# Grouped-query attention on one core: the one-block ScalarE tile of three-block jobs in the transposes' PSUM tile

## The chip, the cores and the metric

The kernel runs on one core of one Trainium2 chip. The metric is the device time of one execution in microseconds (us); lower is better. Times quoted for "the runs" are medians over executions on the chip. The profile is that of a single profiled execution, and its times count from the first instruction of the program (the span). PE is the matrix engine (PEld its weight loads), ACT is ScalarE, DVE is VectorE, POOL is GpSimd, and SP issues most of the transfers. PSUM, where PE writes its results, has eight banks of 512 float32 values in each of 128 partitions.

## The reference

Softmax attention for 8 batches, 512 positions, 32 query heads and 8 key/value heads of dimension 64. Four query heads share one key/value head.

```python
scale = 1.0 / np.sqrt(dim)
K_expanded = np.repeat(K, heads_per_group, axis=2)
V_expanded = np.repeat(V, heads_per_group, axis=2)
scores = np.einsum('bhqd,bhkd->bhqk', Q, K_expanded) * scale
weights = np.exp(scores - np.max(scores, axis=-1, keepdims=True))
weights = weights / (np.sum(weights, axis=-1, keepdims=True) + 1e-10)
output = np.einsum('bhqk,bhkd->bhqd', weights, V_expanded)
```

## The kernel before

The kernel computes exp(score) without subtracting the maximum, sums the weights with a column of ones beside V, divides at the end, and checks at the end that the sums lay in bounds (a general path stands by for other data and isn't run here).

The work is cut into 64 jobs, one for each batch and key/value head. A job has four query heads, taken as two pairs i = 0, 1. For each pair there are four chunks kc of 128 keys and two heads m: 16 blocks of scores in all, each 128 keys by 512 queries, which is one PSUM bank. Two matmuls with 64 rows each make the two blocks (m = 0, 1) of one kc.

The exponential of the 16 blocks is shared out. DVE and POOL together take the first blocks of pair 1: two of them in most jobs, three in every even job from job 10 on (`WIDE`, line 37; 27 such jobs, called three-block jobs here; `taken`, line 183). ScalarE takes the rest in tiles of two blocks (`act_tiles`, `act_tile`, lines 186 and 211). A job with two taken blocks has seven two-block tiles, numbered 0 to 6. A three-block job has an odd number left: its tile 4 has one block (pair 1, kc 1, m 1), the others two.

The eight PSUM banks are held by three pools (lines 84 to 86): two score buffers of two banks each for ScalarE's tiles (`s_pool`, names s_ps), one tile of two banks for DVE's blocks and for transposes (`d_pool`, d_ps), and one of two banks for the products with V (`pv_pool`, pv). A pool's buffer is given out again when all that reads it is done. Since there are two score buffers, the scores of a tile wait until ScalarE has read the tile before the last.

DVE's share of the exponential goes through several steps: u, a scaled and shifted int16 copy of the scores (`exp_d`, line 228); f, the low bits of u (`exp_d2`, line 249); g and w, a correction, in most jobs on POOL (lines 241 and 245, from `correction`); and the sum of u and w, whose bits are the result in pt (`exp_d4`, line 262). Where POOL made w, `exp_d4` of a job is placed in the next job.

All instructions are put out in the order in which the program text names them; each engine works through its own in that order. One turn of the loop over jobs (line 411) for job j puts out, on PE: scores of tiles 0 and 1 and of DVE's first two blocks; the products with V of the job before for pair 0, in two halves with tile 2's scores between them; tile 3's scores; then a d_ps tile with, in its bank 0, eight 128x128 transposes of the Q of a later job (`trans_q`, line 158; two jobs ahead in the stretch concerned); tile 4's scores; and then the products of the job before for pair 1 in three pieces (`cut`, line 432) with the scores of tiles 5 and 6 between them. In a job before a three-block job, the third block of DVE for that job is put in bank 1 of the same d_ps tile (line 484). In a three-block job bank 1 isn't used in this stretch.

On DVE the same turn puts out: u; in some jobs a check of V (`check_v`); `norm` of the job before for pair 0 (reciprocal and o_sb, lines 336 and 340); the copy of the transposes to qt (line 167); `exp_d4` of the job before; f of this job; u of the third block where there is one; `norm` of the job before for pair 1. POOL gets the loads of Q, K and V for later jobs and then g and w. ScalarE gets its seven tiles and nothing else. `norm` frees the pv banks for the next products.

Of the kernel before, what the change touches and what calls it, by code (L numbers as in the profile page):

```python
# [11 lines left out]
FP32 = mybir.dt.float32  # L12
# [46 lines left out]
def fast_path(ctx, tc, Q, K, V, out, flag):  # L59
    nc = tc.nc  # L60
    B, S, H, D = Q.shape
# [5 lines left out]
    NPAIR = HPG // 2  # L67
# [16 lines left out]
    s_pool = ctx.enter_context(tc.tile_pool(name="sps", bufs=2, space=PS))  # L84
# [3 lines left out]
    ident = const_pool.tile([128, 128], BF16, name="ident")  # L88
# [9 lines left out]
    kn, qn, kt, qt = {}, {}, {}, {}  # L98

    def load_k(b, lo=0, hi=KV):  # L100
        if b not in kn:
            kn[b] = knat_pool.tile([128, SC, KV, D], BF16, name="k_nat")
        nc.gpsimd.dma_start(  # L103
            out=kn[b][:, :, lo:hi, :],
            in_=K[b, :, lo:hi, :].rearrange("(sc p) g d -> p sc g d", p=128),
        )


    def load_v(b, lo=0, hi=KV, chunks=range(SC)):
        for sc in chunks:  # L110
            nc.gpsimd.dma_start(  # L111
                out=vt[b % 2][:, sc, lo:hi, 0:D],
                in_=V[b, sc * 128:(sc + 1) * 128, lo:hi, :],
            )
# [6 lines left out]
    def load_q(u, cuts=(0, 2 * HPG)):  # L121
        b, gp = divmod(u, GP)
        h0 = gp * 2 * HPG
        qn[u] = qnat_pool.tile([128, SC, 2 * HPG, D], BF16, name="q_nat")
        for lo, hi in zip(cuts[:-1], cuts[1:]):
            nc.gpsimd.dma_start(  # L126
                out=qn[u][:, :, lo:hi, :],
                in_=Q[b, :, h0 + lo:h0 + hi, :].rearrange("(sc p) h d -> p sc h d", p=128),
            )

    def d_tile():
        return d_pool.tile([128, 2, S], FP32, name="d_ps")
# [15 lines left out]
    def dma_k(b):  # L148
        kt[b] = kt_pool.tile([128, 2, GP, S], BF16, name="kt")
        for sc in range(SC):  # L150
            nc.sync.dma_start_transpose(
                out=kt[b][:, 0, :, sc * 128:(sc + 1) * 128],
                in_=kn[b][:, sc, :, :].rearrange("p g d -> p (g d)"),
            )
        for to, of in ((0, 64), (64, 0)):
            nc.sync.dma_start(out=kt[b][to:to + 64, 1, :, :], in_=kt[b][of:of + 64, 0, :, :])

    def trans_q(j, bank, lo=0, hi=NPAIR):
        u, g = divmod(j, 2)
        ps = bank.bitcast(BF16).rearrange("p (i sc c) -> p i sc c", i=NPAIR, sc=SC)  # L160
        for i in range(lo, hi):
            for sc in range(SC):
                h = g * HPG + 2 * i
                nc.tensor.transpose(ps[:, i, sc, :], qn[u][:, sc, h:h + 2, :], ident)  # L164
        if u not in qt:
            qt[u] = qt_pool.tile([128, 2, NPAIR, S], BF16, name="qt")
        return lambda: nc.vector.tensor_copy(  # L167
            out=qt[u][:, g, lo:hi, :], in_=ps[:, lo:hi, :, :].rearrange("p i sc c -> p i (sc c)")
        )

    def check_v(b, sc):
        n = b * SC + sc
        nc.vector.tensor_reduce(  # L173
            out=okv[:, n:n + 1], in_=vt[b % 2][:, sc, :, 0:D], op=ALU.max, axis=AX.XY,
            apply_absolute_value=True,
        )
# [6 lines left out]
    def taken(j):  # L183
        return 3 if WIDE(j) else 2

    def act_tiles(j):
        every = [(i, kc, m) for i in range(NPAIR) for kc in range(SC) for m in range(2)]
        first = DPAIR * SC * 2
        mine = [n for n in range(len(every)) if not first <= n < first + taken(j)]
        groups = [[n for n in mine if n // 2 == h] for h in range(len(every) // 2)]  # L190
        return [[every[n] for n in group] for group in groups if group]
# [3 lines left out]
    def scores(j, ps, i, kc, m):  # L195
        u, g = divmod(j, 2)
        b, gp = divmod(u, GP)
        keys = kt_first[:, gp, :, :] if b == 0 else kt[b][:, :, gp, :]
        nc.tensor.matmul(  # L199
            ps,  # L200
            keys[64 * m:64 * m + 64, g ^ m, kc * 128:(kc + 1) * 128],
            qt[u][64 * m:64 * m + 64, g, i, :],
            start=True,
            stop=True,
        )

    def open_job(j):
        pt = pt_pool.tile([128, NPAIR, SC, 2, S], FP16, name="pt")
        jobs.setdefault(j, {}).update(pt=pt, pv={})

    def act_tile(j, n):
        group = act_tiles(j)[n]
        i, kc, lo = group[0]
        ps = s_pool.tile([128, 2, S], FP32, name="s_ps")
        for _, _, m in group:
            scores(j, ps[:, m, :], i, kc, m)
        nc.scalar.activation(  # L217
            out=jobs[j]["pt"][:, i, kc, lo:, :], in_=ps[:, lo:, :], func=EXP, scale=scale
        )

    def exp_d(j, lo, hi, ps):
        st = jobs.setdefault(j, {})
        if "u" not in st:
            for name, dtype in (("u", I16), ("f", I16), ("g", BF16), ("w", BF16)):
                st[name] = dve_pool.tile([128, 3, S], dtype, name=name + "16")[:, 0:taken(j), :]
        for n in range(lo, hi):
            scores(j, ps[:, n - lo, :], DPAIR, n // 2, n % 2)
        return lambda: nc.vector.tensor_scalar(  # L228
            out=st["u"][:, lo:hi, :], in0=ps[:, 0:hi - lo, :], scalar1=A_U, scalar2=B_U,
            op0=ALU.mult, op1=ALU.add,  # L230
        )


    def by_pool(j):
        return 3 <= j < NJOB - 1
# [166 lines left out]
    bank = d_tile()  # L402
# [4 lines left out]
    bank = d_tile()  # L407
# [3 lines left out]
    for j in range(NJOB):  # L411
        end = j == NJOB - 1
        last = j - 1
        late = last >= 0
        u, g = divmod(j, 2)
        b, gp = divmod(u, GP)
        open_job(j)
        if j == 1:

            nc.gpsimd.tensor_copy(out=gate, in_=jobs[0]["pt"][0:1, 0, SC - 1, 0, 0:1])  # L420
            load_q(2)
            load_q(3)
        if g == 0 and u >= 1 and u + 3 < NU:
            load_q(u + 3)
        if (gp, g) == (1, 0) and b + 1 < B:
            load_k(b + 1)
        if 3 <= 2 * gp + g < 3 + SC and b + 1 < B:
            load_v(b + 1, chunks=(2 * gp + g - 3,))
        if gp == 2 and g == 0 and b + 1 < B:
            dma_k(b + 1)  # L430

        cut = (4, 18) if taken(j) > 2 else (11, 19)
        act_tile(j, 0)
        if j == 0:
            trans_q(0, bank[:, 1, :], 1, NPAIR)()
            act_tile(j, 1)
            exp_d(j, 0, 2, d_tile())()
        else:
            exp_d(j, 0, 2, d_tile())()
            act_tile(j, 1)  # L440

        if j == 8:
            check_v(0, 0)
        if g == (b < B - 1) and j > 1:
            check_v(b, gp)
        if late:
            pv(last, 0, 0, 16)
        act_tile(j, 2)
        if late:
            pv(last, 0, 16, 32)  # L450
            norm(last, 0)
        act_tile(j, 3)

        reads = []
        if not end:
            bank = d_tile()

            ahead = (j + 1,) if j < 7 else (8, 9) if j == 7 else (j + 2,)
            for n, to in enumerate(ahead):
                if to < NJOB:  # L460
                    reads.append(trans_q(to, bank[:, n, :]))
            if j == 1:
                for swap in range(2):
                    reads.append(first_k(1, swap, bank[:, 1, swap * S // 2:]))
            elif j > 1 and b == 0 and gp + 1 < GP:
                reads.append(first_k(gp + 1, g, bank[:, 1, :]))
        else:
            pv(j, 0, 0, 16)
        for read in reads:
            read()  # L470

        if late and by_pool(last):
            exp_d4(last)
        check_sums()
        exp_d2(j)
        if not by_pool(j):
            exp_d3(j, nc.vector)
            exp_d4(j)
        act_tile(j, 4)
        if late:  # L480
            pv(last, 1, 0, cut[0])
        act_tile(j, 5)
        if not end and taken(j + 1) > 2:
            exp_d(j + 1, 2, taken(j + 1), bank[:, 1:2, :])()
        if late:
            pv(last, 1, *cut)
        act_tile(j, 6)
        if late:
            pv(last, 1, cut[1], 32)
            norm(last, 1)  # L490
            del jobs[last]
        if end:
            pv(j, 0, 16, 32)
            norm(j, 0)
            pv(j, 1, 0, 32)
            norm(j, 1)
# [118 lines left out]
```

## Time and profile before

| | us |
|---|---|
| median of 3 runs | 423.73 |
| lowest and highest of them | 423.38, 423.77 |
| span of the profiled execution | 422.0 |

The profile's page gives the busy time of each engine, then groups of instructions by line, engine and operation with their count, their busy time, the mean length of one in ns, and the idle time of the engine in front of them with what ended it ("<-"). The timeline of an engine lists instructions in order of time as start, length in us, line, operation, output and input tile, and merges equal ones that follow each other ("x14"; the length is then that of the whole stretch). Records of one engine can overlap: the next one begins before the last one has ended, and the idle time counts only stretches that no record covers. Line numbers are those of the kernel before.

The mean clock that PE was granted over the span is 0.984 of the full one.

### The profile page before, as it was taken

The numbers are of one execution on the slowest core, as the hardware profiler recorded it, in microseconds if no ns is written. First come the engines' busy times: TensorE is split into PE (matmuls) and PEld (weight loads), VectorE is DVE, ScalarE is ACT, GpSimd is POOL, SyncE is SP. The second block draws the span as 40 slices with busy tenths as digits, with TensorE's granted clock in tenths as the row PEclk, the third lists the DMA queues.
The fourth block names the chain that finished last, engine by engine and source line by source line (L and its number), as shares of the span: only waits on it lengthen the run. The fifth ranks groups of instructions, "written<-read, shape, count | busy, mean of one in ns | idle before, by whom it ended". The sixth has DMA issues, their size and how long they took to land.

```text
span 422.0 us, 13063 instructions
## 1 busy us (share of the span) xinstructions
PE 385.7 (91%) x5689; PEld 233.6 (55%) x5689; DVE 344.9 (82%) x611; ACT 404.2 (96%) x449; POOL 291.8 (69%) x209
## 2 busy tenths in 40 slices
PE   6889999999999999999999999999999999999983
PEld 2446565555555555555555555555555555555552
DVE  2697788889888888888888888888989888898875
ACT  3899999999999999999999999999999999999992
POOL 8504656778758876787866887677885887666560
PEclk9599999999999999999999999999999999999998
DMA  9996986599967998499964999649996799642223
GB/s 97 177 139 159 217 165 151 70 207 187 191 151 99 216 198 160 133 198 133 229 150 116 206 163 255 157 69 200 157 225 155 122 206 207 148 123 101 102 91 115
DMA packets 91438, 66.95 MB, mean 159 GB/s; under 512 B 52080, under 2 KB 74608, under 8 KB 91376
## 3 DMA queue, kind: packets, MB, share of 16 engines
q0 software_dynamic: 56544, 25.17, 51.1%
q1 hardware_dynamic: 34832, 40.90, 34.5%
q8 instruction: 45, 0.74, 0.7%
q14 instruction: 17, 0.14, 0.1%
HBM read 50.33 MB, written 33.55 MB: 199 GB/s over the span
## 4 chain that ended last, share of the span: by engine, by line
ACT 54%; PE 36%; DVE 6%; issue 1%; POOL 1%; ACTq 0%; DVEq 0%; POOLq 0%
ACT pt L217 54%; PE s_ps L199 17%; PE pv L293 16%; PE d_ps L199 1%; DVE o_sb L340 1%; PE d_ps L164 1%; DVE pt L262 1%; DVE u L228 1%; DVE qt L167 1%; DVE w L245 0%; POOL q_nat L126 0%; DVE kt_first L146 0%; ACTq L217 0%; PE d_ps L143 0%; DVE f L249 0%
## 5 line engine op out<-in xcount | busy, mean ns | idle before, releaser
L217 ACT ACTIVATE pt<-s_ps 128x1024 f16<-128x1024 f32 (+1 forms) x448 | 402.9, 1066 | 9.1 <-PE s_ps L199 9.0
L293 PEld LDWEIGHTS <-pt 128*128 128x128 f16 x4096 | 144.2, 98 | 86.8 <-issue 50.4
L293 PE MATMUL pv<-v,pt 128*128 128x65 bf16 x4032 | 183.2, 195 | 2.6 <-DVE o_sb L340 1.6
L199 PE MATMUL s_ps<-qt,kt 64*128 64x512 bf16 x757 | 152.7, 384 | 19.9 <-ACT pt L217 15.4
L245 POOL TENSOR_TENSOR w<-g,f 128x1024 bf16<-128x1024 bf16 (+1 forms) x60 | 153.7, 2562 | 5.0
L241 POOL TENSOR_SCALAR g<-f 128x1024 bf16<-128x1024 int16 (+1 forms) x60 | 73.9, 1231 | 110.1 <-DVE f L249 110.1
L228 DVE TENSOR_SCALAR u<-d_ps 128x1024 int16<-128x1024 f32 (+1 forms) x91 | 96.2, 1058 | 1.1 <-PE d_ps L199 1.1
L340 DVE TENSOR_TENSOR o_sb<-pv,inv 128x512 f32<-128x512 f32 x125 | 86.5, 692 | 4.5 <-DVE inv L336 0.2
L199 PEld LDWEIGHTS <-kt 64*128 64x128 bf16 x896 | 49.0, 93 | 62.6 <-issue 35.0
L336 DVE RECIPROCAL inv<-pv 128x8 f32<-128x8 f32 x125 | 25.9, 207 | 55.8 <-PE pv L293 55.4
L262 DVE TENSOR_TENSOR pt<-u,w 128x1536 uint16<-128x1536 int16 (+1 forms) x64 | 50.9, 795 | 0.2
L167 DVE COPY qt<-d_ps 128x1024 bf16<-128x1024 bf16 (+1 forms) x65 | 44.3, 683 | 4.5 <-PE d_ps L164 2.9
L164 PE MATMUL d_ps<-ident,q_nat 128*128 128x128 bf16 x512 | 40.1, 222 | 1.1 <-DVE kt_first L146 0.9
L164 PEld LDWEIGHTS <-q_nat 128*128 128x128 bf16 x512 | 29.2, 98 | 15.8 <-issue 15.7
L199 PE MATMUL d_ps<-qt,kt 64*128 64x512 bf16 x139 | 31.4, 376 | 0.3
L249 DVE TENSOR_SCALAR f<-u 128x1536 int16<-128x1536 int16 (+1 forms) x64 | 30.8, 481 | 0.0
L111 POOL DMA_DIRECT2D v<-in_V_dram x32 | 29.0, 910 | 0.4 <-issue 0.4
L126 POOL DMA_DIRECT2D q_nat<-in_Q_dram x34 | 27.4, 806 | 1.5 <-DMA q_nat<-in_Q_dram 1.3
L199 PE MATMUL s_ps<-qt,kt_first 64*128 64x512 bf16 x112 | 23.7, 419 | 4.1 <-ACT pt L217 3.0
L173 DVE TENSOR_REDUCE okv<-v 128x1 f32<-128x512 bf16 x32 | 21.6, 675 | 0.0
L199 PEld LDWEIGHTS <-kt_first 64*128 64x128 bf16 x128 | 8.0, 95 | 12.2 <-issue 8.4
L103 POOL DMA_DIRECT2D k_nat<-in_K_dram x10 | 7.7, 770 | 1.0 <-POOLq L599 0.8
(40 smaller groups left out, 37.6 us busy)
## 6 DMA issues: line engine op xcount, KB each, us to landing
out_dram<-o_sb SPq DMA_DIRECT2D x31, 1024.0 KB, 6.9
q_nat<-in_Q_dram POOLq DMA_DIRECT2D x31, 512.0 KB, 6.3
k_nat<-in_K_dram POOLq DMA_DIRECT2D x7, 512.0 KB, 8.6
v<-in_V_dram POOLq DMA_DIRECT2D x28, 128.0 KB, 7.6
kt<-kt SPq DMA_DIRECT2D x14, 256.0 KB, 4.6
out_dram<-o_sb SPq DMA_DIRECT2D x4, 256.0 KB, 2.4
kt<-k_nat SPq DMA_TRANSPOSE x28, 5.6
v<-in_V_dram POOLq DMA_DIRECT2D x4, 96.0 KB, 7.8
```

The lines of the kernel that those rows point to most:

```text
L111: nc.gpsimd.dma_start(out=vt[b % 2][:, sc, lo:hi, 0:D], in_=V[b, sc * 128:(sc + 1) * 128, lo:hi, :],)
L164: nc.tensor.transpose(ps[:, i, sc, :], qn[u][:, sc, h:h + 2, :], ident)
L167: return lambda: nc.vector.tensor_copy(out=qt[u][:, g, lo:hi, :], in_=ps[:, lo:hi, :, :].rearrange("p i sc c -> p i (sc c)"))
L199: nc.tensor.matmul(ps, keys[64 * m:64 * m + 64, g ^ m, kc * 128:(kc + 1) * 128], qt[u][64 * m:64 * m + 64, g, i, :], start=True, stop=True,)
L217: nc.scalar.activation(out=jobs[j]["pt"][:, i, kc, lo:, :], in_=ps[:, lo:, :], func=EXP, scale=scale)
L228: return lambda: nc.vector.tensor_scalar(out=st["u"][:, lo:hi, :], in0=ps[:, 0:hi - lo, :], scalar1=A_U, scalar2=B_U, op0=ALU.mult, op1=AL ...
L241: engine.tensor_scalar(out=g, in0=f, scalar1=-EXP_F1, scalar2=EXP_K * 2.0 ** (24 * as_bits), op0=ALU.add, op1=ALU.mult,)
L245: engine.tensor_tensor(out=w, in0=g, in1=f.bitcast(FP16) if as_bits else f, op=ALU.mult)
L249: nc.vector.tensor_single_scalar(out=st["f"], in_=st["u"], scalar=1023, op=ALU.bitwise_and)
L262: nc.vector.tensor_tensor(out=st["pt"][:, DPAIR, :, :, :].rearrange("p kc m q -> p (kc m) q")[:, 0:n, :].bitcast(U16), in0=st["u"], in1=st ...
L293: nc.tensor.matmul(st["pv"][i][:, m, qc, :], st["pt"][:, i, kc, m, qc * 128:(qc + 1) * 128], vt[b % 2][:, kc, 2 * gp + g, :], start=(n < 2 ...
L340: nc.vector.tensor_tensor(out=osb[u][:, :, h:h + 2, :].rearrange("p qc m d -> p m qc d"), in0=sums[:, :, :, 0:D], in1=inv[:, :, :, None].t ...
```

## The change

In the turn of a three-block job the one-block tile 4 is put out earlier on PE, straight behind the d_ps tile's allocation and before the transposes, and its scores go to bank 1 of that tile instead of a score buffer. ScalarE's order of tiles is as before. The transposes and their copy by DVE, which work on bank 0 of the same tile, are declared independent of ScalarE's read of bank 1; without that the tile, as one object, would make them wait. Jobs with two blocks taken are unchanged, and so is everything that is computed.

```diff
+    def apart(this, other):
+        if other is not None:
+            tc.declare_no_dep(
+                this.ins, other.ins, reason="the two are in different banks of one tile"
+            )
+        return this
+
-    def trans_q(j, bank, lo=0, hi=NPAIR):
+    def trans_q(j, bank, lo=0, hi=NPAIR, other=None):
...
-                nc.tensor.transpose(ps[:, i, sc, :], qn[u][:, sc, h:h + 2, :], ident)
+                apart(
+                    nc.tensor.transpose(ps[:, i, sc, :], qn[u][:, sc, h:h + 2, :], ident), other
+                )
...
-        return lambda: nc.vector.tensor_copy(
+        return lambda: apart(nc.vector.tensor_copy(
             out=qt[u][:, g, lo:hi, :], in_=ps[:, lo:hi, :, :].rearrange("p i sc c -> p i (sc c)")
-        )
+        ), other)
...
-    def act_tile(j, n):
+    def act_tile(j, n, spare=None):
...
-        ps = s_pool.tile([128, 2, S], FP32, name="s_ps")
+        ps = s_pool.tile([128, 2, S], FP32, name="s_ps") if spare is None else spare
...
-        nc.scalar.activation(
+        return nc.scalar.activation(
...
             bank = d_tile()
+            beside = act_tile(j, 4, bank) if taken(j) > 2 else None
...
-                    reads.append(trans_q(to, bank[:, n, :]))
+                    reads.append(trans_q(to, bank[:, n, :], other=beside))
...
-        act_tile(j, 4)
+        if taken(j) == 2:
+            act_tile(j, 4)
```

## The prediction

> **What bounds the kernel now.** I read the profile's page first, its line of busy times and the list of waits, to find the engine that sets the pace.
>
> ```profile
> span 422.0 us, 13063 instructions
> PE 385.7 (91%) x5689; PEld 233.6 (55%) x5689; DVE 344.9 (82%) x611; ACT 404.2 (96%) x449; POOL 291.8 (69%) x209
> ...
> PE s_ps L199 <- ACT pt L217: 18.4, 60, 0.7
> ...
> ACT pt L217 <- PE s_ps L199: 9.0, 8, 6.2
> ```
>
> ScalarE (ACT) is busy for 404.2 of 422.0 us. The list of waits (total, times, longest) gives it 9.0 us of idle time in 8 stops, 6.2 of it the first one, before any score exists. Nearly all of the other 2.8 lies in the first jobs: grouped by form between 80.7 us and 413 us, from the first three-block job to the last job, its two-block tiles have an idle time of 0.0 before them (count, busy us, mean ns, idle us):
>
> ```profile
> L217 ACT ACTIVATE pt<-s_ps 128x1024 f16<-128x1024 f32 x346 | 320.0, 1085 | 0.0
> ```
>
> The table of busy times by stage says the same of one period of two jobs, from tile 5 of job 30 to tile 4 of job 32 (busy us of PE, PEld, DVE, ACT and POOL behind the length):
>
> ```profile
> 205.62:218.12 12.50, 11.72 (x179) 7.13 (x179) 10.53 (x20) 12.50 (x15) 8.49 (x5) 1.00 0.83 164
> ```
>
> ScalarE is at 12.50 of 12.50. But its records overlap, and a wait shorter than the overlap shows in no idle time. So I went on to ScalarE's own timeline (start, length of the merged stretch, count) and looked at when records end.
>
> ```profile
> 60.77 18.44 ACT L217 ACTIVATE pt<-s_ps 128x1024 f16<-128x1024 f32 x20
> ...
> 203.98 1.17 ACT L217 ACTIVATE pt<-s_ps 128x1024 f16<-128x1024 f32 x1
> ...
> 203.98 1.66 ACT L217 ACTIVATE pt<-s_ps 128x1024 f16<-128x1024 f32 x2
> ...
> 205.62 1.02 ACT L217 ACTIVATE pt<-s_ps 128x1024 f16<-128x1024 f32 x1
> ...
> 206.54 11.59 ACT L217 ACTIVATE pt<-s_ps 128x1024 f16<-128x1024 f32 x13
> ...
> L217 ACT ACTIVATE pt<-s_ps 128x512 f16<-128x512 f32 x27 | 20.3, 753 | 0.0
> ```
>
> The first row is a run of twenty two-block tiles. Its first record is a fresh one of 1.02 us, so nineteen more ends take 18.44 - 1.02 = 17.42 us, 0.917 each. That is ScalarE's pace. A fresh record of 1.02 at a pace of 0.917 must start 0.106 before its predecessor ends, or time is lost.
>
> Around the one-block tile of job 30: tile 3 ends at 203.98 + 1.17 = 205.15, the one-block tile at 203.98 + 1.66 = 205.64, 0.49 later. The next tile starts at 205.62, only 0.02 before that end, is 1.02 long as a fresh one, and ends at 206.64: 1.00 after its predecessor, not 0.917. The tile after that starts at 206.54 with its lead of 0.10 again. There is a hidden stop of nearly 0.1 us. Its size follows better from the period. The tile behind the one-block tile starts at
>
> ```profile
> 80.60 1.02 ACT L217 ACTIVATE pt<-s_ps 128x1024 f16<-128x1024 f32 x1
> ...
> 405.65 1.02 ACT L217 ACTIVATE pt<-s_ps 128x1024 f16<-128x1024 f32 x1
> ```
>
> in the first and in the last of the 27 three-block jobs, 26 periods apart: 325.05 / 26 = 12.502 us. Thirteen two-block tiles and a one-block tile at full pace need 13 x 0.917 + 0.49 = 12.407. So 0.095 us is lost in each period, and 27 x 0.095 = 2.57 us in all.
>
> What ends that stop is on PE's timeline of the same job:
>
> ```profile
> 203.37 0.39 PE L199 MATMUL s_ps<-qt,kt 64*128 64x512 bf16 x2
> 203.69 0.62 PE L164 MATMUL d_ps<-ident,q_nat 128*128 128x128 bf16 x8
> 204.28 0.37 PE L199 MATMUL s_ps<-qt,kt 64*128 64x512 bf16 x1
> 204.58 0.30 PE L293 MATMUL pv<-v,pt 128*128 128x65 bf16 x4
> 205.19 0.39 PE L199 MATMUL s_ps<-qt,kt 64*128 64x512 bf16 x2 [0.31 <-ACT pt L217]
> 205.52 0.61 PE L293 MATMUL pv<-v,pt 128*128 128x65 bf16 x14
> 206.06 0.39 PE L199 MATMUL s_ps<-qt,kt 64*128 64x512 bf16 x2
> ```
>
> Tile 5's scores (205.19) wait 0.31 us for ScalarE: with two score buffers they need the one that tile 3 is read from until 205.15. They end at 205.58, and ScalarE starts on them at 205.62. From tile 3's end to tile 5's start is thus 0.47 us, and the one-block tile in between covers only 0.49 of work, less the 0.106 by which a start should lead.
>
> **The change part by part.** The one-block tile takes bank 1 of the transposes' tile in place of a score buffer. Tile 5's scores then use the buffer of tile 2, which is free a whole tile earlier (tile 3, 0.917 us). Removed: the wait of 0.31. PE reaches tile 5 behind the four pv matmuls. These wait for DVE's o_sb in any case (below), so they stay at 204.58, and from the start of fourteen pv matmuls to the scores behind them is 206.06 - 205.52 = 0.54. Ten fewer are 0.61 - 0.30 = 0.31 less, so four take 0.23, and the scores start at 204.81 and end at 205.20. ScalarE needs them at 205.64 - 0.11 = 205.53. The stop is gone with 0.33 to spare, and tile 6, behind tile 5 on PE, is some 0.3 earlier too, where ScalarE comes only 0.095 earlier.
>
> Added: nothing is computed more or less; one score matmul moves in front of eight transposes. How long it holds them up is shown in the odd job, where a single score matmul also stands behind a pair:
>
> ```profile
> 211.28 0.39 PE L199 MATMUL s_ps<-qt,kt 64*128 64x512 bf16 x2
> 211.49 0.37 PE L199 MATMUL d_ps<-qt,kt 64*128 64x512 bf16 x1
> 211.80 0.57 PE L293 MATMUL pv<-v,pt 128*128 128x65 bf16 x8
> 212.31 0.39 PE L199 MATMUL s_ps<-qt,kt 64*128 64x512 bf16 x2
> ...
> 211.96 1.10 ACT L217 ACTIVATE pt<-s_ps 128x1024 f16<-128x1024 f32 x1
> ```
>
> Pair, single, next kind: 211.80 - 211.28 = 0.52; pair and next kind in the job above: 203.69 - 203.37 = 0.32. So the transposes come 0.20 later. The bounds are 0, if something else held them, and 0.30, the whole slot of the single matmul today (204.58 - 204.28). I take 0.20, since it is the same sequence of shapes. Behind the transposes wait DVE's copy and all that follows in DVE's and POOL's queues:
>
> ```profile
> 203.72 0.69 DVE L340 TENSOR_TENSOR o_sb<-pv,inv 128x512 f32<-128x512 f32 x1
> 204.35 0.69 DVE L167 COPY qt<-d_ps 128x1024 bf16<-128x1024 bf16 x1
> 204.96 0.68 DVE L262 TENSOR_TENSOR pt<-u,w 128x1024 uint16<-128x1024 int16 x1
> 205.56 0.55 DVE L249 TENSOR_SCALAR f<-u 128x1536 int16<-128x1536 int16 x1
> ...
> 211.10 0.95 DVE L262 TENSOR_TENSOR pt<-u,w 128x1536 uint16<-128x1536 int16 x1
> ...
> 206.21 1.47 POOL L241 TENSOR_SCALAR g<-f 128x1536 bf16<-128x1536 int16 x1 [1.32 <-DVE f L249]
> 207.76 3.10 POOL L245 TENSOR_TENSOR w<-g,f 128x1536 bf16<-128x1536 bf16 x1
> ```
>
> The transposes now end at 204.31 and the copy follows at once; they will end near 204.51, the copy starts at 204.55, and exp_d4, f, g and w shift by 0.20. POOL's w ends at 211.06 in place of 210.86. The same w feeds DVE's exp_d4 at 211.10 in the odd job. The hand-over from DVE to POOL takes 206.21 - 206.11 = 0.10; with that much in the other direction exp_d4 starts at 211.16, 0.06 later; with none it isn't moved. Behind exp_d4 stand three of the eight pv matmuls at 211.80 and then tile 6's scores at 212.31. With 0.06 they start at 212.37 and are ready, by the 0.43 from start of scores to start of ScalarE (205.19 to 205.62), at 212.80. ScalarE's tile before ends at 211.96 + 1.10 = 213.06, less the 0.095 that the change brings, and 0.106 earlier the next should start: 212.86. So 0.06 is left; with the upper bound of 0.30 it is missed by 0.04, worth 27 x 0.04 = 1.1 us. The new place costs nothing in the likeliest case, by a small margin.
>
> ScalarE's work itself is the same 448 instructions; the one-block form moves from one PSUM bank to another. The tile's bank 1 is released by ScalarE's read at 205.64, and the next user of the tile, the score blocks of the odd job, comes behind tile 0's scores, which need tile 5's read at 206.6: free. The transposes and the copy carry no wait for ScalarE in the program's order; if one did, PE would stand from 203.9 to 205.7, 1.8 us in each of 27 jobs.
>
> Sum, against the profiled execution: 422.0 - 2.6 = 419.4 us of span. The median of the runs, 423.73, is 1.7 above the span, and I leave that as it is: **421.2 us**.
>
> The pace and the lead come from rows. The Trainium skill, ScalarE: Activation LUTs, section What ACT_TABLE_LOAD costs, has back-to-back ACTIVATEs overlap by about 93 ns, where the rows here give 106. By its figure a lead of 20 ns loses 73, and the sum would be an estimate of 2.0 us, 421.7.
>
> **The rivals.**
>
> *Nothing changes (423.7).* ScalarE's records are back to back, 12.50 of 12.50; if the ends were set by its own pipeline (a long tile behind a short one ending late whatever PE does), the stop would stay. For it: no idle time is listed. Against it: the start at 205.62 is 0.04 after the scores' end, and the record has the 1.02 of a fresh one. The Trainium skill speaks for this rival: Perfetto Trace Analysis, section Identifying the Most-Contended Engine, takes occupancy as a fair measure of how close ScalarE is to its limit, and a stage at 100% would have nothing to give.
>
> *The stop moves to the odd job's tile 6 (421.5 to 423.4).* The POOL chain above delays exp_d4 by 0.10 to 0.15 instead of 0.06; then 0.01 to 0.08 of the 0.095 is lost again: 0.3 to 2.2 us of the gain.
>
> *Slower (425).* The same chain, from copy over f, g, w and exp_d4 to tile 6's scores, decides from the point where it comes 0.06 + 0.06 + 0.095 = 0.215 later at exp_d4: then all is lost. That needs w to end 0.36 later, against the 0.20 that I have and the bound of 0.30. For it: four instructions stand in a row on DVE and two on POOL, and each passes the delay on. Against it: POOL idles 1.32 before g, so nothing adds up there. At 0.05 beyond that point it costs 27 x 0.05 = 1.35: 425.1.
>
> At the end of the kernel the gain of the last period can be lost if something other than ScalarE holds the tail; that is 0.1 us, within the range.
>
> **How the numbers follow.** The forecast gets 0.72 (its own range is 420.8 to 421.7, the spread of the runs shown and the term by the other lead), nothing 0.08, the moved stop 0.13, slower 0.07. The range is 420.7 to 422.9: the low end is the lowest run, 423.38, less 2.57, rounded down; the high end takes in the moved stop with most of the 0.08. 0.2% is 0.85 us, about what can be told from no change. Faster by that is the forecast and nearly all of the moved stop, 0.84; same is the first rival and the rest, 0.10; slower 0.06.
>
> **What would show it.** Right: behind each one-block tile the next record ends 0.917 later, not 1.00; the period falls from 12.50 to 12.41; ScalarE's two-block records grow longer than 1.02 there, since they start early again. PE's wait for ScalarE at tile 5 is gone, 27 x 0.31 of the 18.4 us, in part replaced at other tiles. DVE idles some 0.14 before the copy, for PE, 27 times, and POOL's g starts 0.20 later against ScalarE; exp_d4 of the odd job may wait for POOL's w. Wrong: fresh records of 1.02 at tile 5 still, or at the odd job's tile 6, or any wait of transposes or copy for ScalarE.

## The result, and the profile after

| | before | after |
|---|---|---|
| median (us) | 423.73 | 421.82 |
| lowest and highest of 11 runs | 423.24, 424.90 | 421.29, 422.70 |
| span of the profiled execution | 422.0 | 420.1 |

The ratio is 0.9958, with a 95% interval of 0.9947 to 0.9970: faster by 0.4%.

ScalarE behind the one-block tile of job 30 (ScalarE's timeline of the kernel after: start, length; the one-block tile now reads d_ps and so stands apart):

```profile
203.39 1.08 ACT L226 ACTIVATE pt<-s_ps 128x1024 f16<-128x1024 f32 x1
...
204.29 0.66 ACT L226 ACTIVATE pt<-d_ps 128x512 f16<-128x512 f32 x1
...
204.77 1.10 ACT L226 ACTIVATE pt<-s_ps 128x1024 f16<-128x1024 f32 x1
```

Tile 3 ends at 204.47, the one-block tile at 204.95, tile 5 at 205.87: 0.92 behind it, where it was 1.00. Tile 5's record begins 0.18 before its predecessor's end, so it was ready early; it isn't a fresh one of 1.02 any more. In all 27 three-block jobs tile 5's end now comes 0.92 behind the one-block tile's: the hidden stop is gone.

PE in the same job, from its timeline:

```profile
202.76 0.39 PE L208 MATMUL s_ps<-qt,kt 64*128 64x512 bf16 x2
202.99 0.38 PE L208 MATMUL d_ps<-qt,kt 64*128 64x512 bf16 x1
203.29 0.62 PE L172 MATMUL d_ps<-ident,q_nat 128*128 128x128 bf16 x8
203.85 0.30 PE L302 MATMUL pv<-v,pt 128*128 128x65 bf16 x4
204.08 0.39 PE L208 MATMUL s_ps<-qt,kt 64*128 64x512 bf16 x2
```

Tile 5's scores follow the four pv matmuls with no wait for ScalarE and end at 204.47, 0.30 before ScalarE takes them. The transposes begin 0.53 behind tile 3's scores; that was 0.32.

The gain isn't whole, though. Here are the ends of the one-block tiles of jobs 10 and 62, the first and last of the 27, from ScalarE's timeline:

```profile
79.86 0.84 ACT L226 ACTIVATE pt<-d_ps 128x512 f16<-128x512 f32 x1
...
403.25 0.67 ACT L226 ACTIVATE pt<-d_ps 128x512 f16<-128x512 f32 x1
```

From 80.70 to 403.92 are 323.22 us, 12.432 in each of 26 periods. It was 12.502, and at full pace it would be 12.407. So about 0.025 a period, 0.65 us in all, is lost somewhere else. It lies in six places: at tile 6 of jobs 19, 27, 35, 43, 51 and 59 the next end comes 0.99 to 1.04 after the one before, not 0.917. Job 35 on ScalarE:

```profile
235.89 1.21 ACT L226 ACTIVATE pt<-s_ps 128x1024 f16<-128x1024 f32 x1
...
237.12 1.02 ACT L226 ACTIVATE pt<-s_ps 128x1024 f16<-128x1024 f32 x1
```

The ends are 237.10 and 238.14, 1.04 apart, and the second record is a fresh one. What ends this stop is seen by going back from PE to DVE to POOL, on their timelines in jobs 34 and 35:

```profile
235.84 0.33 PE L302 MATMUL pv<-v,pt 128*128 128x65 bf16 x5
236.49 0.27 PE L302 MATMUL pv<-v,pt 128*128 128x65 bf16 x3 [0.32 <-DVE pt L271]
236.69 0.39 PE L208 MATMUL s_ps<-qt,kt 64*128 64x512 bf16 x2
...
235.47 0.96 DVE L271 TENSOR_TENSOR pt<-u,w 128x1536 uint16<-128x1536 int16 x1 [0.32 <-POOL w L254]
...
232.33 3.11 POOL L254 TENSOR_TENSOR w<-g,f 128x1536 bf16<-128x1536 bf16 x1
```

POOL's w ends at 235.44, exp_d4 starts at 235.47 after a wait of 0.32, three pv matmuls wait 0.32 for it, and tile 6's scores stand behind them. That is the chain of copy, f, g, w and exp_d4 from the prediction. The list of waits has it, with the copy's new wait for the transposes:

```profile
PE s_ps L208 <- ACT pt L226: 13.6, 45, 0.8
...
ACT pt L226 <- PE s_ps L208: 9.1, 7, 6.4
DVE qt L176 <- PE d_ps L172: 6.9, 30, 1.1
...
DVE pt L271 <- POOL w L254: 3.0, 13, 0.3
```

Before the change exp_d4 had no wait for POOL in that list at all.

Why every eighth job? DVE's timeline in job 33, and PE's where jobs 33 and 34 meet, beside the same place two jobs later:

```profile
223.75 0.61 DVE L313 SCALAR_TENSOR_TENSOR ok<-inv,ok 128x128 f32<-128x128 f32 x2
224.28 0.42 DVE L258 TENSOR_SCALAR f<-u 128x1024 int16<-128x1024 int16 x1
224.62 0.68 DVE L237 TENSOR_SCALAR u<-d_ps 128x512 int16<-128x512 f32 x1
...
224.92 0.39 PE L208 MATMUL s_ps<-qt,kt 64*128 64x512 bf16 x2
225.35 0.39 PE L208 MATMUL d_ps<-qt,kt 64*128 64x512 bf16 x2
...
237.51 0.39 PE L208 MATMUL s_ps<-qt,kt 64*128 64x512 bf16 x2
237.73 0.38 PE L208 MATMUL d_ps<-qt,kt 64*128 64x512 bf16 x2
```

In every eighth job (9, 17, 25, 33 and so on) DVE has two more instructions of 0.61 us together, the bounds check of the sums (`check_sums`). The read of the third block behind them ends at 225.30, and PE's next use of that tile, DVE's score blocks of job 34, comes right behind that end: 0.43 behind tile 0's scores, where it is 0.22 two jobs later. PE is late in job 34, and with it the transposes (they begin 1.01 before tile 3 ends on ScalarE, against 1.19 in job 32), the copy, f, g and w. Job 9 has the check too, but job 10's transposes are not late (1.22) and job 11 has no stop. Job 10 is the first three-block job, so nothing is late ahead of it; that this is the reason was not tested.

### The profile page after: what moved, and what is told of

It is laid out like the page before. It is cut to its first block, busy times and chain, and to the rows that moved or that the text cites. A ratio compares the mean times of both kernels' runs of the same rounds, so it can differ in the third digit from the quotient of the medians.

```text
span 420.1 us, 13063 instructions
## 1 busy us (share of the span) xinstructions
PE 382.4 (91%) x5689; PEld 232.7 (55%) x5689; DVE 350.1 (83%) x611; ACT 402.2 (96%) x449; POOL 292.3 (70%) x209
## 4 chain that ended last, share of the span: by engine, by line
ACT 61%; PE 26%; DVE 9%; issue 1%; POOL 1%; ACTq 0%; DVEq 0%; POOLq 0%
ACT pt L226 61%; PE pv L302 11%; PE s_ps L208 10%; PE d_ps L172 3%; DVE o_sb L349 2%; DVE pt L271 2%; DVE u L237 1%; DVE ok L313 1%; PE d_ps L208 1%; DVE f L258 1%; DVE qt L176 1%; DVE w L254 1%; POOL q_nat L126 0%; DVE kt_first L146 0%; PE d_ps L143 0%
## 5 line engine op out<-in xcount | busy, mean ns | idle before, releaser
L226 ACT ACTIVATE pt<-s_ps 128x1024 f16<-128x1024 f32 x421 | 393.2, 1124 | 9.2 <-PE s_ps L208 9.1
L208 PE MATMUL s_ps<-qt,kt 64*128 64x512 bf16 x730 | 142.8, 384 | 15.1 <-ACT pt L226 9.7
L208 PEld LDWEIGHTS <-kt 64*128 64x128 bf16 x896 | 47.9, 93 | 55.4 <-issue 29.4
L208 PE MATMUL d_ps<-qt,kt 64*128 64x512 bf16 x166 | 41.9, 375 | 0.3
L226 ACT ACTIVATE pt<-d_ps 128x512 f16<-128x512 f32 x27 | 18.5, 685 | 0.0
```

The costliest lines, as they stand in the source:

```text
L208: nc.tensor.matmul(ps, keys[64 * m:64 * m + 64, g ^ m, kc * 128:(kc + 1) * 128], qt[u][64 * m:64 * m + 64, g, i, :], start=True, stop=True,)
L226: return nc.scalar.activation(out=jobs[j]["pt"][:, i, kc, lo:, :], in_=ps[:, lo:, :], func=EXP, scale=scale)
```

## The experiments

Theory A: the one-block tile's stop is gone, worth 2.57 us, and 0.65 of it is given back through the chain from the transposes to tile 6 of the odd job. The score in front of the transposes uses up the chain's margin, and `check_sums` in jobs 8k+1 pushes it over in jobs 8k+3. Rival B: in jobs 8k+2 POOL issues a load of K besides that of Q, and in 8k+3 one of V, and these make g and w late whatever PE does.

**The changed kernel once more,** beside the first three experiments.

> The changed kernel once more, on the chip of the three runs beside it, as their measure. Both theories: a ratio to the kernel before of 0.995 to 0.997, and in its profile six stops of ScalarE of about 0.11 us at tile 6 of jobs 19, 27, 35, 43, 51 and 59, and none at tile 5 of the three-block jobs.

Measured: 421.18 us, ratio 0.9938 (0.9922 to 0.9954), a little below the range expected. The six stops are there, 0.06 to 0.11 us long. The runs of one kernel scatter by 1 to 2 us here, more than the 0.65 in question. In the two profiles of this kernel the difference lies ahead of the changed part: the one-block tile of job 10 ends at 80.70 in the first and at 81.47 in the second. The period between jobs 10 and 62, which doesn't depend on the start, is 12.432 in the one and 12.426 in the other. So the experiments that follow are judged by that period.

**The score behind the transposes.**

```diff
-            beside = act_tile(j, 4, bank) if taken(j) > 2 else None
+            beside = []
...
+            if taken(j) > 2:
+                beside.extend(act_tile(j, 4, bank))
```

It stands after the calls of `trans_q`; the copy alone is declared independent, of the score and of ScalarE's read.

> The one-block tile's score stands in bank 1 of the transposes' tile as in the changed kernel, but behind the transposes on PE, where it was before. Theory A (the six stops come through the chain of copy, f, g, w and exp_d4, which the score ahead of the transposes makes 0.20 us later): the copy no longer waits 0.15 us for the transposes, w ends 0.2 us earlier, the six stops of 0.11 go and all of the 2.6 us is gained, ratio 0.9935 to 0.9945. Rival B (the stops come from the loads of K and V on POOL in those jobs, whatever PE does): the six stops stay, ratio as the changed kernel's.

Measured: 421.08 us, ratio 0.9936 (0.9922 to 0.9950). ScalarE's one-block tiles of jobs 10 and 62, and PE in job 30:

```profile
80.72 0.84 ACT L223 ACTIVATE pt<-d_ps 128x512 f16<-128x512 f32 x1
...
403.22 0.91 ACT L223 ACTIVATE pt<-d_ps 128x512 f16<-128x512 f32 x1
...
203.37 0.39 PE L206 MATMUL s_ps<-qt,kt 64*128 64x512 bf16 x2
203.69 0.62 PE L171 MATMUL d_ps<-ident,q_nat 128*128 128x128 bf16 x8
204.24 0.39 PE L206 MATMUL d_ps<-qt,kt 64*128 64x512 bf16 x1
204.56 0.30 PE L299 MATMUL pv<-v,pt 128*128 128x65 bf16 x4
204.79 0.39 PE L206 MATMUL s_ps<-qt,kt 64*128 64x512 bf16 x2
```

From 81.56 to 404.13 are 322.57 us, 12.407 a period: full pace, and no stop of ScalarE between jobs 8 and 62. The transposes are 0.32 behind tile 3's scores again, and tile 5 is as early as in the changed kernel. POOL's loads are untouched, so rival B falls. The bank was worth 2.57 us, the earlier place on PE cost 0.65 of it.

**Without the bounds check in the middle.** What is left out is the comparison of the sums with their bounds, except at the end.

```diff
-        check_sums()
+        full.clear()
         exp_d2(j)
```

> The changed kernel without the bounds check of the sums in the middle of the run (two DVE instructions of 0.61 us together, in jobs 9, 17, 25 and every eighth after them; this part of the check is left out, the outputs do not depend on it). Theory A with its second half (these 0.61 us put DVE behind in jobs 8k+1, PE behind in jobs 8k+2, and with them f and w, so that the margin of the chain is used up in jobs 8k+3 alone): the six stops go, ratio 0.9935 to 0.9945. Rival B (loads on POOL): the six stops stay, no change against the changed kernel.

Measured: 420.92 us, ratio 0.9940 (0.9925 to 0.9956). The six stops are gone, and the same two ends are 322.57 us apart. In the changed kernel both halves of theory A are thus needed for a stop: the 0.2 us of the score, and the 0.6 us of DVE a job earlier. The two act on each other. With the score behind the transposes, the same check leaves job 34's transposes only 0.01 later than job 32's; in the changed kernel it is 0.18, and there exp_d4, which stands in front of the check on DVE in job 33, already begins 0.21 later.

**f first on DVE.**

```diff
+        if taken(j) > 2:
+            exp_d2(j)
         for read in reads:
             read()
...
         check_sums()
-        exp_d2(j)
+        if taken(j) == 2:
+            exp_d2(j)
```

> The changed kernel with f ahead of the copy and of exp_d4 in the three-block jobs' order on DVE; the score stays ahead of the transposes. Theory A: f starts about 1.4 us earlier, POOL's g and w with it, exp_d4 of the odd job never waits for w, the six stops go, ratio 0.9935 to 0.9945; what could spoil it is exp_d4 of the odd job before, 0.55 us later, in front of PE's last eight pv matmuls, which have some 0.3 us of room. Rival B: POOL's loads stand in front of g whatever DVE does, stops stay.

Measured: 441.99 us, ratio 1.0428 (1.0415 to 1.0442). A gain was expected, and 18 us were lost. DVE, POOL and PE in job 42:

```profile
290.75 0.55 DVE L258 TENSOR_SCALAR f<-u 128x1536 int16<-128x1536 int16 x1
291.22 0.68 DVE L176 COPY qt<-d_ps 128x1024 bf16<-128x1024 bf16 x1
291.82 1.87 DVE L271 TENSOR_TENSOR pt<-u,w 128x1024 uint16<-128x1024 int16 x1
...
291.68 1.47 POOL L250 TENSOR_SCALAR g<-f 128x1536 bf16<-128x1536 int16 x1
293.23 3.40 POOL L254 TENSOR_TENSOR w<-g,f 128x1536 bf16<-128x1536 bf16 x1
...
293.74 0.42 PE L302 MATMUL pv<-v,pt 128*128 128x65 bf16 x8 [1.07 <-DVE pt L271]
```

f and POOL are early as meant. But exp_d4, now beside POOL's g, takes 1.87 us where it took 0.68, and PE's last eight pv matmuls wait 1.07 for it. It ends 0.54 after g does, as if it had stood still until g's end at 293.15. So it is in 25 of the 26 three-block jobs that have a copy: exp_d4 takes 1.58 to 1.88 and ends 0.54 behind g. Job 14 is the exception, since exp_d4 begins first there (DVE and POOL):

```profile
107.54 0.68 DVE L271 TENSOR_TENSOR pt<-u,w 128x1024 uint16<-128x1024 int16 x1
...
107.57 1.98 POOL L250 TENSOR_SCALAR g<-f 128x1536 bf16<-128x1536 int16 x1
```

Here exp_d4 takes 0.68, and it is g that takes 1.98 in place of 1.47. Job 15 is also the only odd job from 11 to 61 in which ScalarE has no stop at tile 0; in the others it is 0.51 to 1.09. The next run has exp_d4 ahead of g in every three-block job.

**The copy last on DVE.**

```diff
-        for read in reads:
+        early = reads if taken(j) == 2 else []
+        for read in early:
             read()
...
         exp_d2(j)
+        for read in reads[len(early):]:
+            read()
```

> The changed kernel with DVE's order in the three-block jobs exp_d4, f, copy in place of copy, exp_d4, f. Theory A: f starts 0.7 us earlier, the six stops go, ratio 0.9935 to 0.9945; and if the 18 us that the order f, copy, exp_d4 cost come from exp_d4 (two inputs in SBUF) running beside POOL's g, then here, where exp_d4 ends before g starts, it takes 0.68 us again. Rival (any change of DVE's order there costs, through o_sb or the next use of the tile): slower than the changed kernel by over 1 us.

Measured: 421.29 us, ratio 0.9939 (0.9921 to 0.9957); the six stops are gone, 322.57 us between the two ends. DVE in job 34:

```profile
228.66 0.68 DVE L271 TENSOR_TENSOR pt<-u,w 128x1024 uint16<-128x1024 int16 x1
229.26 0.64 DVE L258 TENSOR_SCALAR f<-u 128x1536 int16<-128x1536 int16 x1
229.82 0.67 DVE L176 COPY qt<-d_ps 128x1024 bf16<-128x1024 bf16 x1
```

exp_d4, ahead of g, takes 0.68 again. f starts some 0.9 earlier than in the changed kernel, and nothing is lost by it. What cost 18 us with f first is what exp_d4 then ran beside.

**A late f, after and before the change.** The same line in both:

```diff
+        if taken(j) > 2:
+            nc.vector.memset(warm, 0.0)
         if late and by_pool(last):
             exp_d4(last)
```

> The changed kernel with one more DVE instruction in each three-block job, a memset of 0.27 us of a buffer that nothing reads any more, between the copy and exp_d4, so that f, g and w come 0.2 to 0.27 us later. Theory A (the chain of copy, f, g, w, exp_d4 and tile 6 of the odd job has next to no margin left, and what it is late is late for the next pair of jobs too): the stop at tile 6 of the odd job comes in nearly every pair, 0.15 to 0.25 us each, and the kernel is slower than before, ratio 1.002 to 1.008. Rival (the chain matters in the six jobs only): 6 x 0.2, ratio about 0.998.

Measured: 427.34 us, ratio 1.0082 (1.0060 to 1.0104), slower than before the change. From the list of waits:

```profile
DVE pt L271 <- POOL w L254: 10.9, 26, 0.6
```

exp_d4 waits for POOL in 26 periods. In the odd jobs from 13 to 61 tile 6 has a stop of 0.38 to 0.39 in the six, and of 0.18 to 0.20 in the others; in job 11 it is 0.11. The period is 12.638. Set beside the changed kernel, these stops show where the room of the chain ends (from the unrounded traces, so rows can differ by 0.01):

| | exp_d4 of the next (odd) job starts behind tile 3's end (us) | stop at that job's tile 6 (us) |
|---|---|---|
| before, job 30 | 5.96 | none |
| after, job 30 | 6.03 | none |
| after, job 20 | 6.06 | none |
| after, job 18 | 6.14 | 0.07 |
| after, job 34 | 6.20 | 0.13 |
| late f, job 30 | 6.26 | 0.19 |
| late f, job 34 | 6.46 | 0.39 |

Up to about 6.07 a later exp_d4 costs ScalarE nothing; beyond that it costs all of the excess.

> The kernel before with the same memset at the same place. Theory A: before the change the same chain has 0.22 us of room behind tile 6's scores and PE waits for ScalarE besides, so the instruction costs nothing or nearly nothing, ratio 0.999 to 1.002. Rival (an instruction of DVE costs its own time wherever it stands): 27 x 0.2, ratio 1.012.

Measured: 423.66 us, ratio 0.9993 (0.9981 to 1.0006). Before the change the same 0.27 us costs nothing. The room of the chain is what the change has spent.

**Without the declaration.**

```diff
-        if other is not None:
+        if False:
```

> The changed kernel without the declaration, so that the transposes and the copy wait for ScalarE's read of the one-block tile. Both theories: the transposes start at that read's end and not at 1.3 to 1.8 us before it; PE stands that long in each of the 27 three-block jobs and has some 0.5 us of room in a pair of jobs, so 0.8 to 1.5 us are lost in each: 445 to 465 us, ratio 1.05 to 1.10. Rival (it would have been hidden): ratio under 1.00.

Measured once: 473.7 us, against a median of 423.63 before. The direction is as expected, the loss larger: 50 us, 1.85 in each three-block job. PE in jobs 28 and 30:

```profile
208.68 0.38 PE L208 MATMUL d_ps<-qt,kt 64*128 64x512 bf16 x1
210.67 0.61 PE L172 MATMUL d_ps<-ident,q_nat 128*128 128x128 bf16 x8 [1.62 <-ACT pt L226]
...
225.34 0.96 PE L172 MATMUL d_ps<-ident,q_nat 128*128 128x128 bf16 x8 [1.70 <-ACT pt L226]
226.09 0.42 PE L302 MATMUL pv<-v,pt 128*128 128x65 bf16 x4
226.45 0.61 PE L208 MATMUL s_ps<-qt,kt 64*128 64x512 bf16 x2
```

The transposes wait 1.62 and 1.70 for ScalarE's read. The room that the expectation subtracted is there at tile 5, where ScalarE stops for 1.25 in most of the jobs. Two things come on top that the expectation lacked. The late copy makes f, w and tile 6 late as well: in 15 of the 26 odd jobs behind such a wait there is a further stop of 0.47. And in the other 11 periods PE is slower behind the wait: two score matmuls take 0.61 and not 0.39.

Three versions thus bring ScalarE to its full pace between jobs 10 and 62: the score behind the transposes, the copy last, and the one without the middle check, which isn't a whole kernel. By the period, the first two beat both kernels (12.407 against 12.432 and 12.426 after, and 12.502 before). By their medians, 421.08 and 421.29 beside 421.18, they can't be told from the changed kernel.

## Why the prediction was right, and where it was off

*The bound, and the hidden stop.* Right. ScalarE's ends set the pace, and 0.095 us were lost in each of 27 periods though its idle time was 0.0. The period forecast for full pace, 12.407, is what the score behind the transposes measured. The sum as written, 13 x 0.917 + 0.49, gives 12.411, which would make the loss 0.091 and 2.46 us in all; with the unrounded spacings of the ends (0.9167 and 0.490) it is 12.407, and the stops measured in the profile before are 0.094 to 0.097. The rival by which the stop is ScalarE's own falls with it: a long tile behind a short one ends 0.92 later when its scores are early.

*Tile 5.* Right. Its scores were to end 0.33 before ScalarE needs them. They end at 204.47, and a start with a lead of 0.11 is due at 204.84: 0.37.

*The transposes 0.20 later.* Right as a sum on PE: 0.53 - 0.32 = 0.21, and the copy idles 0.16 (0.14 forecast). Against ScalarE it was more. In job 30 POOL's w ended 5.71 behind tile 3's end before the change and 5.99 after it, 0.28 later, since tile 3's scores were themselves 0.07 later there.

*The hand-over from POOL to DVE* was taken as 0.10, from the other direction. It is 0.03 (235.44 to 235.47). So exp_d4 of the odd job came 0.07 later in job 30 where 0.06 was forecast, but by luck: 0.08 too little delay and 0.07 too much hand-over nearly cancel.

*"The new place costs nothing in the likeliest case, by a small margin."* The margin was right, and what was taken to use it up was off in size. The prediction lets exp_d4 come 0.12 later before ScalarE loses anything; the table above puts that edge at 6.07 against 5.96 before, 0.11. In job 30 the margin held: no stop in job 31. But not every period is like that one. In job 34 w ended 0.38 later than before the change and not 0.20, and six odd jobs went over, by 0.07 to 0.13 each: 0.65 us. The sign that the prediction named for being wrong, fresh records at the odd job's tile 6, came in those six. Job 34's own rows before the change would have shown part of it: w ends 5.79 behind tile 3's end there, and 0.20 more with the hand-over of 0.03 makes 6.02, close to the edge but no stop yet. What was left out is that the delay feeds itself. A later exp_d4 holds up what stands behind it: on PE the products and tile 6's scores, and on DVE, in every eighth job, the check and the read of the third block. PE then comes later into the next three-block job, and so does the next w, until the room in each pair of jobs has taken it up. Without the check (the run above) the transposes start 1.23 before tile 3's end in job after job; in the changed kernel it is 1.01 in job 34, then 1.14, 1.17 and 1.19, then 1.01 again.

*The sum.* 421.2 was forecast. 421.82 and, in the second set of runs, 421.18 were measured. The first lies just outside the forecast's own range of 420.8 to 421.7 and in that of its second rival, the stop that moves to tile 6 (421.5 to 423.4); the second lies in the forecast's own. The profiles say what happened: both, in part. Between the one-block tiles of jobs 10 and 62 the gain is 325.05 - 323.22 = 1.83 us, which is, to 0.01, the stops of 26 periods, 2.47, less 0.65. The rest of the profile's 422.0 - 420.1 = 1.9 is a start 0.08 longer and an end 0.15 shorter. The rival was priced at 0.3 to 2.2 us for all jobs alike, and came in six. Its working doesn't fit the forecast's margin either: by that margin a delay of 0.10 costs nothing and one of 0.15 costs 0.03, not 0.01 to 0.08.

*The slower rival* did not come, but its mechanism is real: with 0.27 us more on DVE at that place the change is a loss of 0.8%.

## What to carry to other kernels

An engine that is busy all the time can still lose time: where its records overlap, compare the ends of successive records with the pace of an undisturbed stretch, not the idle time, and look for a fresh, short record behind a small tile. When a piece of work is moved ahead of another on a queue, follow what stands behind through all the engines until it comes back, and take the margin from the worst period, not from one. When a margin is small, ask also whether the delay feeds back into the next period. Here the same buffer with the old order on PE kept all of the gain by the period, though its median can't be told from the changed kernel's.

## What the runs showed of the hardware

exp_d4, a tensor_tensor on VectorE with both inputs in SBUF, took 0.68 us away from GpSimd's g and 1.87 us beside it, ending 0.54 after it; the w behind g took 3.40 in place of 3.10. In job 14, where exp_d4 began 0.03 ahead of g, exp_d4 took 0.68 and g 1.98 in place of 1.47. The Trainium skill, SBUF — State Buffer, section Who interferes with whom, says that a VectorE instruction with two SBUF inputs contends with a GpSimd instruction that reads SBUF. The trace agrees.

PE's granted clock fell behind some waits of only 1.6 to 1.7 us in the kernel without the declaration (table by stage: busy us of PE, PEld, DVE, ACT and POOL, then the granted clock):

```profile
209.00:211.00 2.00, 0.38 (x7) 0.40 (x7) 0.49 (x1) 1.62 (x3) 1.10 (x2) 1.00 0.75 63
211.00:215.00 4.00, 4.00 (x48) 2.29 (x44) 2.67 (x6) 2.44 (x3) 1.68 (x2) 0.60 1.25 149
```

Here it is 1.00 in the 2 us that hold the wait and 0.60 in the 4 us after them. Of the 21 waits of 1.6 to 1.7 us in front of the transposes, 11 were followed by a clock of 0.57 to 0.72 over the next 4 us and 10 by one of 1.00; behind the five waits of 1.42 it was 1.00 each time. So the length of the wait alone doesn't decide it; what does was not tried.
